# Relative bias tables gathered on the host and shifted on chip, in place of a table built on chip

## The chip, the core and the metric

One core of one Trainium2 chip runs the whole program. The metric is device microseconds (us) of one execution, the median of several runs. TensorE (PE) does the matrix work, VectorE (DVE), ScalarE (ACT) and GpSimd (POOL) the elementwise work, and SyncE (SP) issues most of the transfers, which run on 16 DMA engines. Each engine carries out its instructions in order and waits on semaphores for the others.

## The reference

One step of an encoder with two layers, over a prompt of 1024 tokens and 8 x 16 sample tokens. Layer 0 is sliding-window attention with a distance penalty; layer 1 is chunked attention over shared K and V with a learned bias per head on the clipped relative distance. Each is followed by a squared-ReLU MLP. What matters here is the bias of layer 1:

```
def relpos_bias(q_pos, k_pos, table):
    rel = jnp.clip(q_pos[:, None] - k_pos[None, :], -MAX_REL, MAX_REL) + MAX_REL
    bias = table.astype(jnp.float32)[:, rel]
    return jnp.where(band_mask(q_pos, k_pos, LEFT_CHUNKS_B)[None], bias, NEG)
...
s = jnp.einsum('bqhgd,bkhd->bhgqk', qg, k) * (HEAD_DIM ** -0.5) + bias
p = jax.nn.softmax(s, axis=-1)
```

The table has 16 heads x 257 distances. A key that is 128 or more behind its query always takes the last entry, the "edge". Softmax doesn't change when the same number is added to a whole row, so a kernel may use table minus edge, and then far keys need no bias at all.

## The kernel before, in words

Tokens go in tiles of 128: eight prompt tiles and one of samples (ST). The stages follow one another on PE: attention of layer 0, output projection, up and down products of the MLP, and the same for layer 1. Every product is made in split form (a high part and the rest), so that each weight or activation block passes through ACT (L128, the high part) and DVE (L134, the rest) or, for the attention's weights, through POOL and DVE (L190). In the down stage, blocks of activations a come from DRAM (hd) and blocks of weights r are added to w; 40 steps of 36 matmuls follow one another.

The bias of layer 1 is made in the first down stage, at step RANK = 20 of 40 (`prep_bias`, `spread_bias`). SP loads the table (tb, L1202). DVE fills fr (L1204) and a tile big of 128 x 1152 (L1205), and forms edge minus table, reversed, in fr (L1206). SP stores fr to DRAM (fd, L1210), then copies it 128 times to rd (L1212, 2048 rows of 1536 bytes), so that a read with a pitch one number short of a row gives a shifted table (`fsrc`). Sixteen small transfers (L1230, L1231) put pieces of it into big for the samples, and L1235 stores big to biasSd.

Layer 1's attention reads them. `bias_b(j)` loads the table of one KV head (four heads, 128 x 1024) from rd with L1627 and masks a corner with a memset (L1628); j = 0 and 1 at the start, 2 and 3 half way. `score_b` and `score_w` add it to the scores, which are made with negated queries, take the minimum, and let ACT compute exp of the minimum minus the score. Each of 16 sample units (`unit`) loads 128 x 288 from biasSd (L558) and does the same in L599 to L600.

The attention opens with K and V of tiles 0, 1 and ST (`K1`): PE projects (L219 to L221), DVE and POOL normalize (kssq L288, kms L290, krs on POOL, kw L293, ks L304), and DVE makes hl, the low part of a tile's hidden state (L134), of the next tile. Meanwhile SP loads four blocks of w_q (L146, raw) and spills hidden states to DRAM (hTd, L1456), all on one queue. A scheduler that simulates the program puts each engine's instructions in order; in the opening those of the attention have a raised priority. In the down stage the order is held by explicit dependences (`behind`, `chain`).

Of the kernel before, what the change touches and what calls it, by code (L numbers as in the profile page):

```python
# [8 lines left out]
F32 = mybir.dt.float32  # L9
F32R = mybir.dt.float32r  # L10
AF = mybir.ActivationFunctionType
ALU = mybir.AluOpType
# [4 lines left out]
P = 128  # L17
# [5 lines left out]
H = 16  # L23
KV = 4
G = 4
# [5 lines left out]
RANK = 20  # L31
# [21 lines left out]
BIG = 1e30  # L53
NREL = 257
# [12 lines left out]
def shape_constants():  # L67
    c = np.zeros((P, C_W), np.float32)
    q = np.arange(P)[:, None]
    k = np.arange(2 * P)[None, :]  # L70
    ba = np.abs(q + P - k).astype(np.float32)
    ba[:64, 192:256] = BIG
    ba[64:, 0:64] = BIG
    c[:, C_BA : C_BA + 256] = ba
    sa = np.full((P, 288), BIG, np.float32)
    i = np.arange(16)
    for hh in range(4):
        for b in range(2):
# [9 lines left out]
    return c  # L88


def halves(t):
# [3 lines left out]
class Build:  # L95
# [443 lines left out]
    def unit(self, up, small, layer, bp, j, v8, gq8, cache_k, cache_v):  # L539
        nc = self.nc  # L540
# [13 lines left out]
        if layer == 0:  # L554
            bias = self.cst[:, C_SA : C_SA + 288]
        else:
            bias = up.tile([P, 288], F32, tag="ub", name="ub")
            nc.sync.dma_start(bias, self.biasSd[j])  # L558
        kp = kc
        self.eng("c").tensor_tensor(kp, kc, gq8.unsqueeze(1).to_broadcast([P, 2, HD]), ALU.mult)  # L560
        if "p" in self.engs:
            yield
            a, b = slice(0, 64), slice(64, 128)
# [16 lines left out]
        s = self.psum("u", [P, 288], "ps_us")  # L580
        for v in range(2):
            nc.tensor.matmul(s, qu[:, v], kb, start=(v == 0), stop=(v == 1))
        mn = small.tile([P, 1], F32, tag="smn", name="smn")
        pn = up.tile([P, P], F32, tag="pn", name="pn")
        nc.gpsimd.memset(pn, 0.0)
        p = up.tile([P, 288], F32, tag="sp", name="sp") if layer == 0 else bias
        l = small.tile([P, 1], F32, tag="sl", name="sl")
        if layer == 0:
            nc.vector.tensor_tensor_reduce(
                s, s, bias, 1.0, self.susink[:, j : j + 1], ALU.add, ALU.min, mn  # L590
            )
# [11 lines left out]
        nc.scalar.activation(p[:, 0:256], p[:, 0:256], AF.Copy, scale=li)  # L603
# [363 lines left out]
    def mlp_down(self, layer, out):  # L967
        nc = self.nc
        tt = nc.vector.tensor_tensor
        wd = self.ins["w_down"][layer].rearrange("(c g h p) n -> g h p c n", g=2, h=2, p=P)  # L970
        with ExitStack() as st:
            self.psum_pools(st, f"dn{layer}", dict(z=(2, 1), c=(6, 1)), dict(c="c"))
            kinds = dict(
                a=([P, 2, 4, 3 * P], F32R), w=([P, 2, 4, 512], F32R), r=([P, 4, 512], F32),
                s=([P, 4, 512], F32), x=([P, D], F32),
# [11 lines left out]
            for n, tags in enumerate(DOWN_HOME):  # L987
                pool = self.pool(st, f"d{n}_{layer}")
                for t in tags.split():
                    if t == "bias":  # L990
                        self.bias_tiles(pool)
                        pool.tile([P, 248], F32, tag="pad", name="pad")
                    elif t[0] == "+":
# [130 lines left out]
                    chain(z)  # L1124
            late = iter(self.late)
            for n, (s, p, g, first, final, reads, _) in enumerate(seq):
                if layer == 0 and n == RANK:
                    self.prep_bias(self.dp)
                if layer == 0 and n == RANK + 4:
                    self.spread_bias(self.dp)  # L1130
                if n + AHEAD < total:
                    load_w(n + AHEAD)
                split_h(n + 1)
# [6 lines left out]
                a, w = aa.pop(n), ws.pop(n)  # L1140
                adds, whole = {}, {}
                for o, v in reads:
                    if o not in opened:
# [3 lines left out]
                        z = take(f"o{no % 2}")  # L1147
# [3 lines left out]
                for i in range(3):  # L1151
                    if i == 2 and n + 2 in total_of:
                        chain(total_of[n + 2])
                    c = slice(i * P, i * P + P)
                    z = [
                        self.mm3(
                            banks[i], a[:, 0, k, c], a[:, 1, k, c], w[:, 0, k], w[:, 1, k],
                            first and k == 0, k == 3,
                        )
                        for k in range(4)  # L1160
                    ]
                    self.follow(z[0][0], z[-1][1])
                    for o, v in reads:
# [6 lines left out]
                        t = PARTS[o // 2][i]  # L1170
# [22 lines left out]
    def bias_tiles(self, pool):  # L1193
        self.tb = pool.tile([H, NREL], F32, tag="tb", name="tb")
        self.fr = pool.tile([H, 384], F32, tag="fr", name="fr")
        self.big = pool.tile([P, KV, 288], F32, tag="big", name="big")

    def prep_bias(self, dp):
        nc = self.nc
        with ExitStack() as st:  # L1200
            tb, fr, big = self.tb, self.fr, self.big
            a = nc.sync.dma_start(tb, self.ins["rel_bias_b"][0])  # L1202
            self.behind(self.sp, a)
            self.behind(self.dve, nc.vector.memset(fr, 0.0))  # L1204
            self.behind(self.dve, nc.vector.memset(big, BIG))  # L1205
            nc.vector.tensor_scalar(  # L1206
                fr[:, 127:383], tb[:, 256:0:-1], -1.0, tb[:, 256:257], ALU.mult, ALU.add
            )
            fd = dp.tile([H, 384], F32, tag="fd", name="fd")
            nc.sync.dma_start(fd, fr)  # L1210
            rd = dp.tile([H, P, 384], F32, tag="rd", name="rd")
            nc.sync.dma_start(rd, fd[0:H].unsqueeze(1).to_broadcast([H, P, 384]))  # L1212
            ra = rd[0:H]

            def fsrc(h, off, n, nh, hs, w):
                return bass.AP(
                    tensor=ra.tensor, offset=ra.offset + h * P * 384 + 127 + off,
                    ap=[[383, n], [hs * P * 384, nh], [1, w]],
                )

            self.fsrc = fsrc

    def spread_bias(self, dp):
        nc, big, fsrc = self.nc, self.big, self.fsrc
        for h4 in range(G):
            for b in range(2):
                r = slice(h4 * 32 + b * 16, h4 * 32 + b * 16 + 16)
                c = 256 + b * 16
                for z in (
                    nc.sync.dma_start(big[r, :, b * P : b * P + P], fsrc(h4, 0, 16, KV, G, P)),  # L1230
                    nc.sync.dma_start(big[r, :, c : c + 16], fsrc(h4, P, 16, KV, G, 16)),  # L1231
                ):
                    self.behind(self.sp, z)
        self.biasSd = dp.tile([KV, P, 288], F32, tag="biasSd", name="biasSd")
        nc.sync.dma_start(self.biasSd[0:KV].rearrange("j p c -> p j c"), big)  # L1235

    def prep_gains(self):
        nc, I = self.nc, self.ins
# [130 lines left out]
    def attention(self, layer):  # L1369
        nc, I = self.nc, self.ins  # L1370
        A = layer == 0
# [16 lines left out]
        with ExitStack() as st:  # L1388
# [4 lines left out]
            self.pad(st, f"smpad{layer}", 32 if A else 256)  # L1393
# [3 lines left out]
            self.pad(st, f"ringpad{layer}", 168 if A else 64)  # L1397
# [226 lines left out]

            def bias_b(j):
                b = ring.tile([P, G, 256], F32, tag="biasB", name="biasB", bufs=cfg["bias_bufs"])
                nc.sync.dma_start(b, self.fsrc(j * G, 0, P, G, 1, 256))  # L1627
                nc.vector.memset(b[0:64, :, 192:256], BIG)  # L1628
                self.biasB[j] = b

# [146 lines left out]
            for s in range(2 * NT):  # L1777
# [54 lines left out]
def make_plan(tail, second):  # L1832
# [16 lines left out]
AFTER = mybir.DependencyInfo(mybir.DependencyClass.NoSync, mybir.DependencyReason.DATA)  # L1849
EARLY = (300, 150, 110, 90)  # L1850
DOWN_HOME = (
    "s1", "r0", "o0", "+512", "s0", "o1", "+512", "r3", "x5", "x6", "x7", "bias", "r4", "r5", "+384", "x8", "x0", "x2", "+640",
    "a0", "x1", "x3", "x4", "r6", "a1", "a2", "w0", "w1", "r7", "r8", "r9", "r10",
)
TAIL = 6
# [56 lines left out]
```

## Time and profile before

| What | Value |
|---|---|
| Runs before | 2350.42, 2356.03, 2356.86 us (median 2356.03) |
| Span of the profiled execution, first to last instruction | 2349.6 us |
| Its own time | not listed apart; the shortest run lies 0.8 us above the span |
| PE busy | 2273.2 us, 97% |
| DVE busy | 1718.3 us, 73% |
| ACT busy | 1332.0 us, 57% |
| POOL busy | 644.7 us, 27% |
| SP's DMA queue q1 | 188816 packets, 283.58 MB, 37.8% of the 16 engines' span |
| Granted PE clock, mean | 0.993 |
| First down stage, where the bias is made | about 963 to 1017 us of the span |
| Opening of the second attention | about 1131 to 1184 us |

A row of the timeline has the start, the duration, the engine with its line, the operation, the tiles written and read, and in brackets how long the engine was idle before it and what ended that. "SPq" rows are transfers being issued. "PEclk" is the granted clock as a share of full speed. The counts of DMA packets by size sum over the 16 DMA engines; the transfers' own marks of completion, 4 bytes each, are counted among them.

### The profile page before, as it was taken

The page shows a single profiled execution, that of the slowest core. Times are in us where ns is not written, and L with a number is a line of the kernel's source. Part 1 is how long each engine was busy: PE and PEld are TensorE (multiplying, and loading weights), DVE is VectorE, ACT ScalarE, POOL GpSimd, SP SyncE. Part 2 cuts the span into 40 slices and gives each one's busy share as a digit, 9 for nine tenths or more (in the row PEclk, how much of TensorE's full clock was granted, in tenths as well). Part 3 has the DMA queues.
Part 4 walks back from the last instruction along what each step waited for, and adds up shares of the span by engine and source line. Part 5 has one row for each costly group of instructions (what it writes and reads, how often), then busy time and mean ns, then how long its engine had stood idle before and what let it go on. Part 6 is the DMA issues. An engine that isn't in the chain of part 4 may idle for free.

```text
span 2349.6 us, 33397 instructions
## 1 busy us (share of the span) xinstructions
PE 2273.2 (97%) x11429; PEld 1899.3 (81%) x11429; DVE 1718.3 (73%) x3075; ACT 1332.0 (57%) x2684; POOL 644.7 (27%) x950
## 2 busy tenths in 40 slices
PE   8999999899999999999899899999899999999999
PEld 6787877788888888778778778887888888888887
DVE  6888786766656578898577776877666566678987
ACT  3777674555555555344377666665655555555443
POOL 4434332313213111002433444345132132210011
PEclk9999999999999999999999999999999999999999
DMA  7435546234334687848654656555243343877567
GB/s 262 128 103 177 166 141 208 89 122 162 132 112 152 218 231 174 272 142 206 191 157 114 190 151 180 166 172 186 72 162 132 114 160 113 276 212 197 183 165 198
DMA packets 226715, 392.70 MB, mean 167 GB/s; under 512 B 51592, under 2 KB 126288, under 8 KB 226448
## 3 DMA queue, kind: packets, MB, share of 16 engines
q1 hardware_dynamic: 188816, 283.58, 37.8%
q0 software_dynamic: 36432, 102.26, 16.0%
q10 hardware_dynamic: 1296, 4.72, 0.5%
q8 instruction: 90, 1.47, 0.3%
q14 instruction: 81, 0.66, 0.1%
HBM read 236.51 MB, written 156.85 MB: 167 GB/s over the span
## 4 chain that ended last, share of the span: by engine, by line
PE 73%; DVE 11%; DMA 8%; ACT 3%; issue 2%; POOL 2%; SPq 1%; ACTq 0%; DVEq 0%; POOLq 0%
PE ps_c L745 7%; PE ps_c L746 7%; PE ps_c L747 7%; PE ps_x L745 5%; PE ps_x L747 5%; PE ps_x L746 5%; PE ps_mm L219 3%; PE ps_mm L221 3%; PE ps_mm L220 3%; PE ps_y L747 2%; PE ps_y L746 2%; PE ps_y L745 2%; PE ps_tr L326 2%; DMA a<-hd 2%; DVE w L134 1%
## 5 line engine op out<-in xcount | busy, mean ns | idle before, releaser
L746 PE MATMUL ps_c<-w,a 128*128 128x512 f32 x960 | 374.0, 390 | 3.9 <-DVE w L134 3.9
L745 PE MATMUL ps_c<-w,a 128*128 128x512 f32 x960 | 374.1, 390 | 3.2 <-ACT o L1165 1.7
L747 PE MATMUL ps_c<-w,a 128*128 128x512 f32 x960 | 373.5, 389 | 0.0
L910 POOL DMA_DIRECT2D hd<-h x272 | 149.4, 552 | 594.3 <-ACT h L819 378.4
L745 PEld LDWEIGHTS ps_c<-w,a 128*128 128x128 f32 x960 | 180.2, 188 | 42.9 <-issue 2.7
L746 PEld LDWEIGHTS ps_c<-w,a 128*128 128x128 f32 x960 | 180.2, 188 | 42.7 <-DVE w L134 5.6
L747 PEld LDWEIGHTS ps_c<-w,a 128*128 128x128 f32 x960 | 180.2, 188 | 37.4
L128 ACT CAST a<-a 128x1536 fp32r<-128x1536 f32 x80 | 118.6, 1483 | 154.6 <-DMA a<-hd 154.6
L219 PE MATMUL ps_mm<-w,hh 128*128 128x512 f32 x432 | 173.9, 403 | 12.8 <-ACT hh L128 5.4
L221 PE MATMUL ps_mm<-w,hl 128*128 128x512 f32 x432 | 172.4, 399 | 1.4 <-DVE hl L134 1.2
L220 PE MATMUL ps_mm<-w,hh 128*128 128x512 f32 x432 | 171.4, 397 | 0.3
L134 DVE TENSOR_TENSOR a<-a 128x1536 fp32r<-128x1536 f32 x80 | 140.6, 1757 | 40.6 <-ACT a L128 40.5
L745 PE MATMUL ps_x<-sx,w 128*128 128x512 f32 (+1 forms) x408 | 157.8, 387 | 4.5 <-ACT h L866 2.7
L128 ACT CAST w<-ru 128x512 fp32r<-128x512 f32 (+1 forms) x160 | 109.9, 708 | 84.4 <-PE ps_y L746 32.0
L128 ACT CAST w<-s 128x2048 fp32r<-128x2048 f32 x56 | 107.1, 1912 | 88.2 <-DVE s L1062 78.8
L747 PE MATMUL ps_x<-sx,w 128*128 128x512 f32 (+1 forms) x408 | 154.2, 378 | 0.3 <-DVE w L134 0.3
L746 PE MATMUL ps_x<-sx,w 128*128 128x512 f32 (+1 forms) x408 | 154.1, 378 | 0.0
L134 DVE TENSOR_TENSOR w<-s,w 128x2048 fp32r<-128x2048 f32 x56 | 128.2, 2289 | 32.3 <-ACT w L128 32.0
L1182 POOL DMA_DIRECT2D xp<-o x28 | 36.2, 1294 | 411.6 <-ACT o L1165 391.0
L134 DVE TENSOR_TENSOR w<-ru,w 128x512 fp32r<-128x512 f32 (+1 forms) x160 | 129.7, 813 | 14.8 <-ACT w L128 14.7
L134 DVE TENSOR_TENSOR ptl<-ps_tr,pth 128x512 fp32r<-128x512 f32 x180 | 122.5, 685 | 21.2 <-ACT pth L128 17.5
L818 ACT ACTIVATE h<-h 128x512 f32<-128x512 f32 (+1 forms) x102 | 61.9, 607 | 122.1 <-DVE h L868 93.0
(274 smaller groups left out, 6152.9 us busy)
## 6 DMA issues: line engine op xcount, KB each, us to landing
a<-hd SPq DMA_DIRECT2D x80, 768.0 KB, 6.2
hd<-h POOLq DMA_DIRECT2D x272, 192.0 KB, 2.5
ru<-in_w_up SPq DMA_DIRECT2D x64, 512.0 KB, 3.9
r<-in_w_down SPq DMA_DIRECT2D x32, 1024.0 KB, 9.8
xp<-o POOLq DMA_DIRECT2D x28, 768.0 KB, 9.5
o<-oTd SPq DMA_DIRECT2D x50, 256.0 KB, 3.9
x<-xp SPq DMA_DIRECT2D x23, 512.0 KB, 5.5
xp<-xo SPq DMA_DIRECT2D x18, 512.0 KB, 2.9
```

The costliest lines, as they stand in the source:

```text
L128: a = nc.scalar.copy(hi, src)
L134: return a, e.tensor_tensor(lo, src, hi.bitcast(F32), ALU.subtract)
L219: nc.tensor.matmul(ps, a, w[:, 0, k, :], start=(k == 0), stop=False)
L220: nc.tensor.matmul(ps, a, w[:, 1, k, :], start=False, stop=False)
L221: self.lp = nc.tensor.matmul(ps, b, w[:, 0, k, :], start=False, stop=(k == KC - 1))
L326: self.lp = nc.tensor.transpose(pt[:, i, :], get(i), self.ident)
L745: a = mm(ps, ah, bh, start=first, stop=False, skip_group_check=True)
L746: mm(ps, ah, bl, start=False, stop=False, skip_group_check=True)
L747: return a, mm(ps, al, bh, start=False, stop=last, skip_group_check=True)
L818: a = nc.scalar.activation(t, src, AF.Relu)
L910: return lambda p, z: self.nc.gpsimd.dma_start(self.hd[c // 4][:, p, c % 4], z)
L1182: nc.gpsimd.dma_start(dst, z, accum_op=ALU.add)
```

## The change

The host gathers two tables from the input, without arithmetic other than a fill value: rel_p, per KV head 128 x 4 x 256 numbers, and rel_s, per KV head 128 x 288. `prep_bias`, `spread_bias` and `bias_tiles` go; their place in SBUF is kept by a gap of 2048 numbers. `bias_b` loads rel_p, and DVE subtracts it from the edge, relf, on chip. relf, 128 x 16, is loaded once at the start of the second attention, repeated over all partitions. The sample unit adds rel_s in its plain sign, takes the maximum, and negates it with one more small instruction.

```diff
             bias = up.tile([P, 288], F32, tag="ub", name="ub")
-            nc.sync.dma_start(bias, self.biasSd[j])
+            nc.sync.dma_start(bias, self.ins["rel_s"][j])
...
-            nc.vector.tensor_tensor_reduce(s, s, bias, 1.0, BIG, ALU.add, ALU.min, mn)
-            nc.scalar.activation(p, s, AF.Exp, bias=mn, scale=-1.0, accum_out=l)
+            nc.vector.tensor_tensor_reduce(s, bias, s, 1.0, -BIG, ALU.subtract, ALU.max, mn)
+            nm = small.tile([P, 1], F32, tag="snm", name="snm")
+            nc.vector.tensor_scalar(nm, mn, -1.0, None, ALU.mult)
+            nc.scalar.activation(p, s, AF.Exp, bias=nm, accum_out=l)
...
-                if layer == 0 and n == RANK:
-                    self.prep_bias(self.dp)
-                if layer == 0 and n == RANK + 4:
-                    self.spread_bias(self.dp)
...
-                nc.sync.dma_start(b, self.fsrc(j * G, 0, P, G, 1, 256))
+                nc.sync.dma_start(b, I["rel_p"][j])
+                edge = relf[:, j * G : j * G + G].unsqueeze(2).to_broadcast([P, G, 256])
+                nc.vector.tensor_tensor(b, edge, b, ALU.subtract)
                 nc.vector.memset(b[0:64, :, 192:256], BIG)
...
                 self.biasB = {}
+                relf = ring.tile([P, H], F32, tag="relf", name="relf")
+                nc.sync.dma_start(relf, I["rel_bias_b"][0, :, NREL - 1].partition_broadcast(P))
                 bias_b(0)
...
+def relative_tables(rel):
+    q = np.arange(P)[:, None]
+    at = np.clip(q + P - np.arange(2 * P)[None, :], -128, 128) + 128
+    p = rel[:, at].reshape(KV, G, P, 2 * P).transpose(0, 2, 1, 3)
```

The order of instructions moves at three places that the prediction speaks of. First, SP's queue at the opening of the second attention, from gq on (raw is w_q, hTd the spilled hidden states, biasB the table of one KV head). Before:

```order
L627 DMA gq<-in_g_q_b 128x64
L1627 DMA biasB<-rd 128x4x256
L1456 DMA hTd_114<-hh 128x512
L1456 DMA hTd_114<-hl 128x512
L1456 DMA hTd_115<-hh 128x512
L146 DMA raw<-in_w_q_b 128x2x512
```

After, with the line numbers of the changed kernel:

```order
L643 DMA gq<-in_g_q_b 128x64
L1641 DMA relf<-in_rel_bias_b 128x16x1
L1592 DMA biasB<-in_rel_p 128x1024
L1421 DMA hTd_114<-hh 128x512
L1421 DMA hTd_114<-hl 128x512
L160 DMA raw<-in_w_q_b 128x2x512
```

The load of relf stands ahead of the first table, and the third block of w_q has moved ahead of a spill.

Second, DVE at the same time, from the first K tile's sum of squares on (kssq, kms, kw and ks belong to the K normalization, VS to V, hl to the sample tile's hidden state). Before:

```order
L288 TENSOR_REDUCE kssq<-kw 128x4
L1628 MEMSET biasB 64x4x64
L290 TENSOR_SCALAR kms<-kssq,ex 128x4
L293 TENSOR_TENSOR kw<-kw,krs 128x256
L304 TENSOR_TENSOR ks<-kw,gkq 128x256
L279 SCALAR_TENSOR_TENSOR VS<-ps_mm,rx,VS 128x4x64
L134 TENSOR_TENSOR hl<-ps_n,hh 128x512 x2
```

After:

```order
L302 TENSOR_REDUCE kssq<-kw 128x4
L1594 TENSOR_TENSOR biasB<-relf,biasB 128x1024
L304 TENSOR_SCALAR kms<-kssq,ex 128x4
L1595 MEMSET biasB 64x4x64
L293 SCALAR_TENSOR_TENSOR VS<-ps_mm,rx,VS 128x4x64
L307 TENSOR_TENSOR kw<-kw,krs 128x256
L148 TENSOR_TENSOR hl<-ps_n,hh 128x512
```

The subtraction has come in ahead of kms, and VS stands ahead of kw.

Third, DVE in the first down stage, where the table was made (x are output tiles, a and w the split blocks). Before:

```order
L1204 MEMSET fr 16x384
L1205 MEMSET big 128x1152
L134 TENSOR_TENSOR a_9985<-a_9985 128x1536
L134 TENSOR_TENSOR w_10050<-s_9994,w_10050 128x2048
L1062 TENSOR_TENSOR s_10053<-r_9935,r_9987 128x2048
L1206 TENSOR_SCALAR fr<-tb 16x256
```

After, the three rows on fr and big are gone and the others stand in the same order; on SP the loads and stores of tb, fd, rd, big and biasSd are gone likewise. In the second attention all engines' rows are interleaved anew; outside it nothing else moves.

More of the change, by code (lines that the diff above doesn't have):

```diff
@@ L88, in shape_constants @@
     return c
+def relative_tables(rel):
+    q = np.arange(P)[:, None]
+    at = np.clip(q + P - np.arange(2 * P)[None, :], -128, 128) + 128
+    p = rel[:, at].reshape(KV, G, P, 2 * P).transpose(0, 2, 1, 3)
+    s = np.full((KV, P, 288), -BIG, np.float32)
+    i = np.arange(16)[:, None]
+    for hh in range(G):
+        for b in range(2):
+            r = slice(hh * 32 + b * 16, hh * 32 + b * 16 + 16)
+            s[:, r, b * P : (b + 1) * P] = rel[hh::G][:, at[:16, :P]]
+            s[:, r, 256 + b * 16 : 256 + b * 16 + 16] = rel[hh::G][:, i - i.T + 128]
+    return np.ascontiguousarray(p), s
 def halves(t):
@@ L989, in mlp_down @@
                 for t in tags.split():
[L990 to L993, printed above, removed]
+                    if t[0] == "+":
                         pool.tile([P, int(t[1:])], F32, tag="gap", name="gap")
@@ L1191, in mlp_down @@
                         load_h(m)
[L1193 to L1235, printed above, removed]
     def prep_gains(self):
@@ L1392, in attention @@
             small = self.pool(st, f"sm{layer}", 4 if A else 3)
-            self.pad(st, f"smpad{layer}", 32 if A else 256)
+            self.pad(st, f"smpad{layer}", 32 if A else 232)
             hpool = self.pool(st, f"ht{layer}")
@@ L1396, in attention @@
             ring = self.pool(st, f"ring{layer}")
-            self.pad(st, f"ringpad{layer}", 168 if A else 64)
+            self.pad(st, f"ringpad{layer}", 168 if A else 48)
             apool = self.pool(st, f"att{layer}", 2)
@@ L1851 @@
 DOWN_HOME = (
-    "s1", "r0", "o0", "+512", "s0", "o1", "+512", "r3", "x5", "x6", "x7", "bias", "r4", "r5", "+384", "x8", "x0", "x2", "+640",
+    "s1", "r0", "o0", "+512", "s0", "o1", "+512", "r3", "x5", "x6", "x7", "+2048", "r4", "r5", "+384", "x8", "x0", "x2", "+640",
     "a0", "x1", "x3", "x4", "r6", "a1", "a2", "w0", "w1", "r7", "r8", "r9", "r10",
@@ L1898 @@
     given["eye"] = np.eye(P, dtype=np.float32)
+    given["rel_p"], given["rel_s"] = relative_tables(np.asarray(inputs["rel_bias_b"])[0])
     for name, a in given.items():
```

## The prediction

> **What bounds the kernel now.** I read the page first, for who is busy and what the chain that ended last is made of.
>
> ```profile
> span 2349.6 us, 33397 instructions
> PE 2273.2 (97%) x11429; PEld 1899.3 (81%) x11429; DVE 1718.3 (73%) x3075; ACT 1332.0 (57%) x2684; POOL 644.7 (27%) x950
> PE 73%; DVE 11%; DMA 8%; ACT 3%; issue 2%; POOL 2%; SPq 1%; ACTq 0%; DVEq 0%; POOLq 0%
> ```
>
> TensorE (PE) is busy 97% of the span and none of its work changes. So an edit can only move the 76.4 us in which PE is idle (2349.6 − 2273.2): it gains at most the idle time that it caused, and it loses whatever it puts between PE and its operands. Next I asked for busy time by stretch, at the places that the change touches: the first down stage, the opening of the second attention, and its steady part.
>
> ```profile
> 955.00:1030.00 75.00, 70.77 (x309) 57.32 (x308) 64.75 (x55) 29.52 (x20) 0.00 (x0) 1.00 0.66 220
> 1142.00:1150.00 8.00, 8.00 (x31) 6.42 (x30) 5.27 (x11) 1.83 (x5) 1.37 (x2) 0.81 0.99 303
> 1150.00:1158.00 8.00, 8.00 (x42) 6.71 (x41) 5.55 (x16) 2.85 (x10) 3.63 (x6) 1.00 0.99 324
> 1200.00:1620.00 420.00, 403.14 (x2206) 334.92 (x2206) 318.19 (x868) 278.39 (x766) 173.80 (x234) 0.99 0.53 160
> ```
>
> The columns are length, then PE, PEld, DVE, ACT and POOL busy, the granted clock, the DMA share and GB/s. In the down stage around the removed preparation PE is busy 70.77 of 75 us. In the opening (1142 to 1158) PE is busy throughout, and so are the DMA engines, at 0.99: every packet put into the queue there delays what stands behind it. In the steady part PE is idle for 16.9 of 420 us.
>
> **What the removal gives.** These are the times at which PE waited between 955 and 1030, from the timeline:
>
> ```profile
> 972.85 0.50 PE L746 MATMUL ps_c<-w,a 128*128 128x512 f32 x1 [1.06 <-DVE w L134]
> 989.75 0.47 PE L745 MATMUL ps_c<-w,a 128*128 128x512 f32 x1 [0.52 <-DVE x L1177]
> 1000.16 0.50 PE L746 MATMUL ps_c<-w,a 128*128 128x512 f32 x1 [1.74 <-DVE w L134]
> ```
>
> And these are the rows of the preparation, with the one on which the third wait hangs:
>
> ```profile
> 967.40 0.38 DVE L1204 MEMSET fr<- 16x384 f32 x1
> 967.97 1.02 DVE L1205 MEMSET big<- 128x1152 f32 x1 [0.19 <-issue]
> 994.63 1.48 ACT L128 CAST a<-a 128x1536 fp32r<-128x1536 f32 x1 [3.41 <-DMA a<-hd]
> rd<-fd SPq DMA_DIRECT2D x1, 3072.0 KB, 15.7
> ```
>
> The two memsets took VectorE (DVE) from 967.40 to 968.99, 1.59 us ahead of the split of w whose end released PE at 972.85. Without them that wait of 1.06 us is covered. The 0.52 us at 989.75 has the same origin, since DVE ran late from there on: taken as gone as well. The 1.74 us at 1000.16 come from an activation block a that ACT got only at 994.63, while the 3 MB copy rd<-fd shared the queue with it: gone too. The gain is 1.06 + 0.52 + 1.74 = 3.3 us. Its bounds are 0 (something else is late next) and 3.3 (PE wasn't idle for longer). The other removed transfers (tb, fd, sixteen big<-rd, biasSd) have no PE wait behind them.
>
> **What the addition costs: one small load in a full queue.** The new relf load takes one number per head out of rows that lie 1028 bytes apart and repeats it for 128 partitions. That is 128 x 16 = 2048 pieces of 4 bytes, 8 KB in all. SP issues it behind gq and ahead of the first bias table, a split block of hidden state, and the last two blocks of w_q. The trace has no such load of 2048 pieces, so I bound it by counted packets. First the four ssink loads at the start (4-byte pieces repeated over partitions, 512 in all), the stretch in their midst, and then gk and gq at the very place of relf (rows repeated over partitions), and one load of 256 rows that aren't repeated:
>
> ```profile
> DMA packets 880, 0.74 MB, mean 143 GB/s; under 512 B 603, under 2 KB 603, under 8 KB 880
> ...
> DMA packets 135, 0.00 MB, mean 0 GB/s; under 512 B 135, under 2 KB 135, under 8 KB 135
> ...
> DMA packets 565, 0.53 MB, mean 313 GB/s; under 512 B 299, under 2 KB 505, under 8 KB 564
> ...
> GB/s 0 0 0 0 0 0 0 0 0 0 26 85 119 85 128 188 196 230 197 205 205 213 137 120 35 290 0 0 0 0 0 0 0 0 0 0 0 0 0 0
> DMA packets 273, 0.07 MB, mean 61 GB/s; under 512 B 272, under 2 KB 272, under 8 KB 272
> ```
>
> - ssink, from 16.5 to 21.7 us: 603 packets under 512 bytes in 5.2 us, 116 per us, so relf would hold the queue for 2048 / 116 = 17.7 us.
> - In its midst, 17.75 to 19.5: 135 packets in 1.75 us, 77 per us, which would make 26.5 us.
> - gk and gq, 1146.5 to 1148.2: 299 in 1.7 us, 176 per us, so 11.6 us.
> - kc, 78.8 to 80.0: 272 in the 16 of 40 slices of 0.03 us that moved bytes, 567 per us, so 3.6 us.
>
> I take 11.6 us, from gk and gq: relf is repeated over partitions as they are, and stands next to them on the same queue. The ends 3.6 and 17.7 stay for the range. That a slow small load holds back what is behind it shows at the start:
>
> ```profile
> 16.12 0.39 SPq L146 DMA_DIRECT2D raw<-in_w_qkv_a  x1
> 16.87 0.35 SPq L1456 DMA_DIRECT2D hTd<-hh  x1
> 22.32 0.16 DVE L1367 TENSOR_TENSOR susink<-ssink,rsl 128x4 f32<-128x4 f32 x1 [3.39 <-DMA ssink<-in_sink_a]
> ```
>
> The block raw was issued at 16.12 and the spill hTd at 16.87, yet from 17.75 to 19.5 not one of the 135 packets was as large as 512 bytes: ssink's pieces were in front.
>
> [...]
>
> **Who waits for it.** DVE takes the first subtraction (biasB from relf, 128x1024) just ahead of kms of the first K tile. DVE works in order, so everything behind that waits too: the K normalizations, VS, and hl of the sample tile, which PE needs next. The rows of before at that place:
>
> ```profile
> 1143.96 0.70 SPq L1627 DMA_DIRECT2D biasB<-rd  x1
> DMA to landing us min/median/max: 5.7/6.1/6.5
> 1151.18 0.27 DVE L1628 MEMSET biasB<- 64x256 f32 x1
> 1151.38 0.20 DVE L290 TENSOR_SCALAR kms<-kssq,ex 128x4 f32<-128x4 f32 x1
> 1152.70 0.42 DVE L293 TENSOR_TENSOR kw<-kw,krs 128x256 f32<-128x256 f32 x1 [1.13 <-POOL krs L292]
> 1154.62 0.48 DVE L279 SCALAR_TENSOR_TENSOR VS<-ps_mm,rx,VS 128x256 fp32r<-128x256 f32 x1 [1.03 <-ACT VS L278]
> 1155.11 1.29 DVE L134 TENSOR_TENSOR hl<-ps_n,hh 128x512 fp32r<-128x512 f32 x2
> 955.07 1.75 DVE L134 TENSOR_TENSOR a<-a 128x1536 fp32r<-128x1536 f32 x1
> ```
>
> The table lands at 1143.96 + 6.1 = 1150.1, about 1 us before DVE asks for it. With relf ahead it lands at 1150.1 + D. The subtraction takes about 1.2 us (128x512 took 0.65 each in the pair at 1155.11, 128x1536 took 1.75). Behind it come kms 0.20, the memset 0.27, VS 0.48 and kw 0.42, with some 0.35 of waiting for POOL in between, 2.9 us in all. So hl starts at 1153.0 + D instead of 1155.11: the delay is D − 2.1 us, because DVE had two waits there (1.13 and 1.03) that the new wait swallows. PE was never idle in this stretch and its row of work is in order, so it stops for 11.6 − 2.1 = 9.5 us. The last w_q blocks are delayed as well, through the same queue, but no further than this.
>
> A stop that long costs PE more than its length:
>
> ```profile
> 1140.86 0.76 PE L219 MATMUL ps_mm<-w,hh 128*128 128x512 f32 x1 [5.43 <-ACT hh L128]
> 1145.66 0.40 PE L219 MATMUL ps_mm<-w,hh 128*128 128x512 f32 x1
> 1146.35 0.40 PE L219 MATMUL ps_mm<-w,hh 128*128 128x512 f32 x1
> 1180.08 0.89 PE L433 MATMUL ps_sn<-KT,qT 128*128 128x128 f32 x6 [2.24 <-DVE qT L134]
> 1170.00:1184.00 14.00, 11.76 (x71) 10.09 (x70) 8.99 (x22) 7.16 (x15) 5.24 (x4) 1.00 0.35 106
> ```
>
> After 5.43 us of idleness the first four groups of three matmuls took 1145.66 − 1140.86 = 4.80 us, where the next one took 0.69: 4.80 − 4 x 0.69 = 2.0 us lost, at a granted clock of 0.81. After 2.24 us of idleness the clock stayed at 1.00. So 2.0 us more where the stop is nearer 5 us, nothing where it is under 2.2.
>
> **The small edits.** The other three subtractions are 1.2 us of DVE each:
>
> ```profile
> 1381.42 0.27 DVE L1628 MEMSET biasB<- 64x256 f32 x1 [0.27 <-DMA biasB<-rd]
> 1393.96 0.27 DVE L1628 MEMSET biasB<- 64x256 f32 x1 [2.14 <-DMA biasB<-rd]
> 1150.21 0.15 DVE L204 TENSOR_SCALAR vx<-xssq 128x1 f32<-128x1 f32 x1
> PE ps_utp L607 <- ACT ub L603: 0.3, 1, 0.3
> ```
>
> For the later two tables DVE waited already, up to 2.14 us, and the list of PE's waits names no biasB: covered by PE's queued work, 0; without that cover 2.4 us. The second subtraction stands between two halves of the last w_q block, behind the same queue: inside the 9.5. The negation in each of 16 sample units costs 0.15 us as the 128x1 row; PE waited only once on that chain, 0.3 us: I take 0.5 us, bounds 0 and 2.4. Reading in_rel_s instead of biasSd moves the same bytes: 0. The scheduler also interleaves the second attention anew; PE's work is the same, and of its 16.9 us idle there a third may come or go: 0, give or take 5.
>
> **The sum.** −3.3 + 9.5 + 2.0 + 0.5 = +8.7 us on the profiled execution. Its span is 2349.6; the shortest of the three runs, 2350.42, lies 0.8 above that, and the median, 2356.03, 6.4 above it. Added to the median: 2364.7 us. About 0.3%, 7.1 us, is what a measurement of this kernel can tell from no change.
>
> **Rivals.**
> - *The small load is quick* (not slower than before): relf goes at kc's pace, 3.6 us. Then hl is only 1.5 us late, PE's clock stays up, and −3.3 + 1.5 + 0.5 = −1.3 gives 2354.7; wholly hidden it is −2.8 and 2353.2. For it: relf's 16 sources lie 1028 bytes apart, where ssink's lie next to each other. Against: none of the repeated loads ran at that pace. It decides below a relf of 5 us; the loss passes 0.3% only above 10 us (D − 2.9 = 7.1). [...]
> - *ssink's own pace*: D = 17.7, so −3.3 + 15.6 + 2.0 + 0.5 = +14.8 and 2370.8. For it: the same piece size and kind. Against: it ran at the very start.
> - *The new interleaving decides*: half of the 16.9 us idle in the steady part gained or doubled up. With a quick relf that is −2.8 − 8.4, 2344.8; on top of the forecast +17.1, 2373.1. Nothing in the trace speaks for either sign.
>
> **How the numbers follow.** Chances: forecast (D from 8 to 15, so +5 to +12) 0.48; quick load 0.27; ssink's pace 0.15; interleaving 0.10, half to each sign. Of the forecast's share two thirds lie above 10 us, 0.31 slower and 0.17 within 0.3%. Slower: 0.31 + 0.15 + 0.05 = 0.51. Within: 0.17 + 0.27 = 0.44. Faster: 0.05. The range runs from a little under the hidden load to a little over ssink's pace with some loss: 2352 to 2373.
>
> **What would show it.** Right: DVE waiting around 1150 for relf or biasB for some 10 us, PE idle about as long before the sample tile's K projection and a granted clock under 1 behind it, and about 2 us or less of PE idle between 955 and 1030. Wrong: a wait at that subtraction under 3 us (quick load), PE waits in the down stage that stay, or a gap in the opening that is made up again by 1200.

## The result and the profile after

The change took 2367.03 us in the median (2361.89 to 2371.51, six runs), the kernel before 2356.29 beside it: a ratio of 1.0045 with a 95% interval from 1.0029 to 1.0062, slower by 10.7 us. The forecast was 2364.7. The time came out about as forecast, but the profile shows that it got there by another way. The page of the changed kernel, its span, its engines' busy time and the chain of work that ended last:

```profile
span 2363.6 us, 33385 instructions
PE 2282.2 (97%) x11429; PEld 1904.6 (81%) x11429; DVE 1721.5 (73%) x3092; ACT 1332.7 (56%) x2684; POOL 647.7 (27%) x950
PE 79%; DVE 9%; DMA 6%; ACT 2%; issue 2%; SPq 1%; POOL 0%; ACTq 0%; DVEq 0%; POOLq 0%
```

The profiled execution took 2365.41 us. TensorE's busy time rose by 9.0 us (from 2273.2) with the same 11429 matmuls: the same work ran on a slower clock for a while (a granted clock of 0.990 in the mean, where before had 0.993). The next views ask in which stage. First the down stage and the edge's load, by windows (same columns as in the prediction), then the packets of the second window:

```profile
955.00:1030.00 75.00, 74.51 (x329) 61.33 (x328) 69.62 (x55) 33.44 (x22) 0.00 (x0) 1.00 0.51 174
1139.70:1142.80 3.10, 3.10 (x16) 2.55 (x15) 3.10 (x4) 0.50 (x1) 1.38 (x2) 1.00 0.55 61
```

```profile
DMA packets 2274, 0.19 MB, mean 61 GB/s; under 512 B 2244, under 2 KB 2244, under 8 KB 2273
```

TensorE got through 329 matmuls in the 75 us where it did 309 before: 20 x 74.51 / 329 = 4.5 us gained, as an estimate. And the 2244 small packets around the edge's load, which has 128 x 16 = 2048 pieces, passed in 3.1 us with TensorE busy all the time; 2034 of them were of 4 bytes. The first K product on TensorE, SP's queue and the first subtraction, from the timeline:

```profile
1132.94 0.47 PE L233 MATMUL ps_mm<-w,hh 128*128 128x512 f32 x1 [1.47 <-ACT hh L142]
...
1138.27 0.43 SPq L1641 DMA_DIRECT2D relf<-in_rel_bias_b  x1
1138.74 3.49 SPq L1592 DMA_DIRECT2D biasB<-in_rel_p  x1
...
1146.32 1.23 DVE L1594 TENSOR_TENSOR biasB<-relf,biasB 128x1024 f32<-128x1024 f32 x1 [1.84 <-DMA biasB<-in_rel_p]
```

VectorE waited 1.84 us for the first table, not some 10, and TensorE didn't stop for it. TensorE's wait ahead of the first K product shrank to 1.47 us from 5.43. So far the changed kernel is ahead. It loses all of that, and more, in the steady part of the second attention. I take that part from the first ps_sn product to the first product of the output projection, and behind it to the 200th product of the next up stage: both hold the same numbers of matmuls in all of these kernels, give or take missing records. Before, then after:

```profile
1180.10:1618.10 438.00, 421.13 (x2316) 350.88 (x2317) 332.71 (x923) 292.14 (x808) 180.35 (x249) 0.99 0.53 162
1618.10:1730.30 112.20, 103.26 (x606) 89.88 (x605) 80.16 (x121) 65.75 (x130) 38.77 (x44) 0.97 0.40 134
```

```profile
1171.30:1628.60 457.30, 430.48 (x2315) 356.06 (x2316) 334.52 (x941) 292.14 (x808) 183.32 (x249) 0.97 0.51 155
1628.60:1744.00 115.40, 104.21 (x605) 91.05 (x604) 78.66 (x121) 65.70 (x130) 40.53 (x44) 0.96 0.38 130
```

The steady part takes 457.3 us in place of 438.0. Of the 19.3 us, 457.30 - 430.48 - (438.00 - 421.13) = 9.9 are idleness, and 430.48 - 421.13 = 9.4 are the same matmuls on a granted clock of 0.97 in place of 0.99. The profile doesn't say whether the added work or the order did this; the experiments have to.

### The profile page after: what moved, and what is told of

It reads as the page before. It is cut to its first block, busy times and chain, and to the rows that moved or that the text cites. A ratio compares the mean times of both kernels' runs of the same rounds, so it can differ in the third digit from the quotient of the medians.

```text
span 2363.6 us, 33385 instructions
## 1 busy us (share of the span) xinstructions
PE 2282.2 (97%) x11429; PEld 1904.6 (81%) x11429; DVE 1721.5 (73%) x3092; ACT 1332.7 (56%) x2684; POOL 647.7 (27%) x950
## 3 DMA queue, kind: packets, MB, share of 16 engines
q8 instruction: 90, 1.47, 0.3%
## 4 chain that ended last, share of the span: by engine, by line
PE 79%; DVE 9%; DMA 6%; ACT 2%; issue 2%; SPq 1%; POOL 0%; ACTq 0%; DVEq 0%; POOLq 0%
PE ps_c L761 8%; PE ps_c L763 8%; PE ps_c L762 8%; PE ps_x L761 5%; PE ps_x L763 5%; PE ps_x L762 5%; PE ps_mm L233 3%; PE ps_mm L234 3%; PE ps_mm L235 3%; PE ps_y L763 2%; PE ps_tr L340 2%; PE ps_y L761 2%; PE ps_y L762 2%; PE ps_mm L190 2%; PE ps_mm L192 1%
## 5 line engine op out<-in xcount | busy, mean ns | idle before, releaser
L142 ACT CAST pth<-ps_tr 128x512 fp32r<-128x512 f32 x180 | 105.1, 594 | 50.2 <-PE ps_tr L340 40.8
```

Of the source, the lines that this page charges most:

```text
L142: a = nc.scalar.copy(hi, src)
```

## The experiments

Two theories stood against each other. *Order*: the scheduler interleaved the second attention anew, and in the new order TensorE stops more often; the added work is nearly free. *Work*: the subtractions, the negations and the edge's load cost the time. A third, *table*, was kept beside them: the tables gathered on the host land later than those built on chip. To part them I tied rows to a given order: between neighbours in the wanted order of TensorE and of VectorE a dependence is added that carries no semaphore, so that it holds the scheduler alone and makes nothing wait on the chip. Other engines stay free, and nearly fall into the same order.

```diff
+    def pin(self):
+        by = {i.name: i for b in self.nc.main_func.blocks for i in b.instructions}
+        for rows in PINS.values():
+            for a, b in zip(rows, rows[1:]):
+                self.tc.add_manual_dep(by[f"I-{b}"], f"I-{a}", AFTER, reason="pin")
```

All results together. "Moved" is the smallest number of TensorE's rows to take out so that the others stand as in the kernel before. Ratios are to runs of the kernel before on the same chip, whose medians were 2355.65 to 2357.82 us.

| Kernel | Moved | Median us | Ratio, 95% interval |
|---|---|---|---|
| the change | 395 | 2367.03 | 1.0045 [1.0029, 1.0062] |
| removal alone | 9 | 2347.12 | 0.9955 [0.9939, 0.9970] |
| the change, old order | 0 | 2349.68 | 0.9966 [0.9952, 0.9980] |
| removal alone, the change's order | 395 | 2367.08 | 1.0043 [1.0026, 1.0059] |
| the change, unit in its old form | 272 | 2362.31 | 1.0017 [1.0005, 1.0029] |
| the change, TensorE's old order only | 0 | 2352.91 | 0.9984 [0.9969, 0.9998] |
| the change, old order in the late part | 300 | 2355.60 | 0.9995 [0.9982, 1.0008] |
| the change, old order in the early part | 95 | 2358.21 | 1.0002 [0.9985, 1.0018] |
| the change, old order, four edge loads | 0 | 2358.85 | 1.0015 [1.0000, 1.0029] |
| before, one more row per unit | 535 | 2369.12 | 1.0058 [1.0044, 1.0072] |
| the same, old order | 0 | 2354.04 | 0.9994 [0.9982, 1.0006] |
| additions alone | 535 | 2372.47 | 1.0067 [1.0052, 1.0082] |
| the change, negation on GpSimd | 342 | 2357.03 | 1.0004 [0.9995, 1.0014] |

**Work and order taken apart.** The removal alone, in nearly the old order (the fill value of the samples' table and two paddings change with it and aren't shown):

```diff
-                edge = relf[:, j * G : j * G + G].unsqueeze(2).to_broadcast([P, G, 256])
-                nc.vector.tensor_tensor(b, edge, b, ALU.subtract)
...
-                relf = ring.tile([P, H], F32, tag="relf", name="relf")
-                nc.sync.dma_start(relf, I["rel_bias_b"][0, :, NREL - 1].partition_broadcast(P))
...
-            nc.vector.tensor_tensor_reduce(s, bias, s, 1.0, -BIG, ALU.subtract, ALU.max, mn)
-            nm = small.tile([P, 1], F32, tag="snm", name="snm")
-            nc.vector.tensor_scalar(nm, mn, -1.0, None, ALU.mult)
-            nc.scalar.activation(p, s, AF.Exp, bias=nm, accum_out=l)
+            nc.vector.tensor_tensor_reduce(s, s, bias, 1.0, BIG, ALU.add, ALU.min, mn)
+            nc.scalar.activation(p, s, AF.Exp, bias=mn, scale=-1.0, accum_out=l)
```

> The removal alone: the table is no longer built in the first down stage and the attention loads the gathered tables, but there is no load of the edge, no subtraction and no negation, and the sample unit keeps its old form (so the shift by the edge and the sign of the bias are left out of the computation). TensorE's rows stand as before, but for 9 moved ones. Order theory (the new interleaving costs some 19 us in the second attention): the down stage gives its 5 us and nothing is lost later, 2351 us, from 2346 to 2353. Work theory (the four subtractions, the 16 negations and the edge's load cost the 19 us): the same, 2351. Table theory (the tables gathered on the host land later than the ones built on chip): 2360 or more.

The whole change with the rows of before (PINS from the kernel before):

> The whole change, with the rows of TensorE and VectorE in the second attention tied to the order that they had before (the added rows stand at their places in the program). Order theory: 2351 us plus at most 3 for the added work, 2350 to 2355. Work theory: as slow as the change itself, 2364 to 2369. Table theory: 2364 to 2369 too.

And the removal alone with the rows of the change (PINS from the changed kernel):

> The removal alone as above (shift and sign left out), with the rows of TensorE and VectorE in the second attention tied to the order that the whole change has. Order theory: nearly as slow as the whole change, 2363 to 2368. Work theory: 2351, as the removal alone. Table theory: 2360 or more, as the removal alone.

2347.12, 2349.68 and 2367.08 us: the order theory holds in all three (the second lies 0.3 us under its 2350 to 2355), and the work and table theories fall. The change's order costs 20.0 us (2367.08 - 2347.12) with none of the added work in it and 17.3 (2367.03 - 2349.68) with all of it, and the added work costs 2.6 us (2349.68 - 2347.12) in the old order, which these intervals, of about 0.14% to each side, don't tell from nothing. The steady part and what follows it, in the whole change with the old order:

```profile
1172.30:1607.10 434.80, 419.40 (x2317) 347.89 (x2317) 335.49 (x941) 292.34 (x808) 179.70 (x249) 1.00 0.53 163
1607.10:1718.30 111.20, 103.34 (x604) 89.98 (x603) 79.58 (x121) 65.62 (x130) 38.53 (x44) 0.97 0.41 135
```

and in the removal alone with the change's order:

```profile
1179.60:1625.40 445.80, 424.28 (x2317) 350.96 (x2317) 331.56 (x923) 291.18 (x808) 180.62 (x249) 0.99 0.52 159
1625.40:1743.40 118.00, 105.08 (x605) 91.60 (x603) 78.35 (x121) 65.34 (x130) 39.30 (x44) 0.94 0.38 127
```

The columns of VectorE (335.49 against 331.56 us) show that the first does more work and the second less, and yet the first takes 546.0 us for both stretches and the second 563.8. These are single executions, and the first of them took 2341.08 us, 8.6 under its median, so the size of the gap is read from the medians. One thing stays open: the change itself takes 572.7 us for these stretches, 8.9 more than the removal in the same order, but reaches them 8.3 us earlier. So that the added work is nearly free is shown for the old order only.

**What a worse order looks like.** TensorE's waits of over 1 us between 1300 and 1352 in the changed kernel:

```profile
1305.47 0.63 PE L340 MATMUL ps_tr<-identr,p 128*128 128x128 f32 x4 [1.69 <-DVE KT L148]
1314.99 0.62 PE L447 MATMUL ps_sf<-KT,qT 128*128 128x384 f32 x2 [1.25 <-ACT p L484]
1319.53 0.77 PE L233 MATMUL ps_mm<-w,hh 128*128 128x512 f32 x1 [2.85 <-DMA hh<-hTd]
1334.37 0.50 PE L233 MATMUL ps_mm<-w,hh 128*128 128x512 f32 x1 [1.08 <-DMA hh<-hTd]
1350.75 0.53 PE L596 MATMUL ps_us<-kb,qu 128*128 128x288 f32 x2 [1.46 <-DVE KT L148]
```

With the old order the same stretch has two:

```profile
1313.36 0.47 PE L233 MATMUL ps_mm<-w,hh 128*128 128x512 f32 x1 [1.45 <-DMA hh<-hTd]
1325.24 0.47 PE L233 MATMUL ps_mm<-w,hh 128*128 128x512 f32 x1 [1.16 <-DMA hh<-hTd]
```

The first of the five can be read off VectorE's timeline. KT is the low part of a K tile, in two halves; the transposes of p (ps_tr) at 1305.47 start once the second is done. In the changed kernel:

```profile
1300.86 0.42 DVE L148 TENSOR_TENSOR KT<-ps_q,KT 64x256 fp32r<-64x256 f32 x1
1301.50 1.17 DVE L204 SCALAR_TENSOR_TENSOR w<-raw,gcol,w 128x512 fp32r<-128x512 f32 x1 [0.23 <-POOL w L199]
1302.76 0.11 DVE L471 MEMSET ps_sf<- 64x64 f32 x1
1302.78 0.47 DVE L493 TENSOR_TENSOR l<-l 128x2 f32<-128x2 f32 x1
1303.17 0.77 DVE L204 SCALAR_TENSOR_TENSOR w<-raw,gcol,w 128x512 fp32r<-128x512 f32 x1
1303.86 0.47 DVE L293 SCALAR_TENSOR_TENSOR VS<-ps_mm,rx,VS 128x256 fp32r<-128x256 f32 x1
1304.25 0.54 DVE L472 TENSOR_REDUCE mnb<-ps_sf 128x1 f32<-128x384 f32 x1
1304.71 0.15 DVE L494 RECIPROCAL li<-l 128x2 f32<-128x2 f32 x1
1304.89 0.43 DVE L148 TENSOR_TENSOR KT<-ps_q,KT 64x256 fp32r<-64x256 f32 x1
```

and in the old order:

```profile
1298.13 0.42 DVE L148 TENSOR_TENSOR KT<-ps_q,KT 64x256 fp32r<-64x256 f32 x1
1298.47 0.47 DVE L475 CUSTOM_DVE_ANT_0 ps_sn<-ps_sn,biasB,mnb 128x256 f32<-128x256 f32 x1
1298.97 0.08 DVE L475 DVE_READ_ACCUMULATOR2_ANT mnb<- 128x1 f32 x1
1299.08 0.43 DVE L148 TENSOR_TENSOR KT<-ps_q,KT 64x256 fp32r<-64x256 f32 x1
```

The halves start 0.95 us apart in the old order. In the new one seven rows stand between them, two of them parts of the weights' preparation (L204), and they start 4.03 us apart. None of these rows is new; they only stand elsewhere. All five waits come back in the removal with the change's order, which has none of the added work: 1.69, 1.23, 3.27, 1.13 and 1.83 us.

**Which engine, and which part of the stage.** TensorE's rows alone tied to the old order:

> The whole change, with TensorE's rows alone tied to the order that they had before; VectorE's are left to the scheduler (93 of them moved against before, where the whole change moves 278). If TensorE's order is what costs: as fast as with both tied, 2348 to 2354 us. If it is VectorE's order: between 2356 and 2367. Work theory (by now unlikely): 2367.

2352.91 us: 14.1 of the 17.3 us that both together bring come back with TensorE's rows alone. Next, one part of the stage in the old order, the other in the new (PINS cut where the two orders hold the same rows so far):

> The whole change; TensorE and VectorE keep the new order up to about 1508 us of the span and the old one behind it, to the end of the second attention. By the profiles, the stretch from there into the next up stage took 231.3 us in the whole change and 220.5 with the old order. If the loss is spread over the stage, this kernel gains that part, 10.8 of 2367: 2356, from 2353 to 2360. If all of it comes from the early part (where the first tables and the first units stand): 2367. If all of it comes from the late part: 2350.

> The whole change; TensorE and VectorE keep the old order up to about 1508 us of the span and the new one behind it. If the loss is spread: what the late part doesn't explain, 17.3 - 10.8 = 6.5 us less than 2367, so 2360.5, from 2357 to 2364, and the gains of this kernel and of its counterpart add up to some 17. If the early part is all: 2350; if the late part is all: 2367.

The late part brings 2367.03 - 2355.60 = 11.4 us (10.8 were expected from the profiles), the early part 8.8 (6.5 expected); the sum is 20.2 where both bring 17.3, as near as the intervals allow. So the loss is spread over the stage. Waits come and go with their part. In the kernel whose early part is new, the wait of 1.69 us of the changed kernel is back:

```profile
1311.38 0.63 PE L340 MATMUL ps_tr<-identr,p 128*128 128x128 f32 x4 [1.69 <-DVE KT L148]
```

and in the one whose late part is new, the longest stop stands at the end of the output projection (the change itself stops there for 4.7 us),

```profile
1651.54 1.12 PE L708 MATMUL ps_n<-identr,x 128*128 128x128 f32 x4 [6.10 <-DVE sx L148]
```

where the change in the old order waits less than half as long:

```profile
1634.02 1.25 PE L708 MATMUL ps_n<-identr,x 128*128 128x128 f32 x8 [2.80 <-DVE sx L148]
```

**What sets the order.** The sample unit in its old form, without the negation:

```diff
-            nc.vector.tensor_tensor_reduce(s, bias, s, 1.0, -BIG, ALU.subtract, ALU.max, mn)
-            nm = small.tile([P, 1], F32, tag="snm", name="snm")
-            nc.vector.tensor_scalar(nm, mn, -1.0, None, ALU.mult)
-            nc.scalar.activation(p, s, AF.Exp, bias=nm, accum_out=l)
+            nc.vector.tensor_tensor_reduce(s, s, bias, 1.0, BIG, ALU.add, ALU.min, mn)
+            nc.scalar.activation(p, s, AF.Exp, bias=mn, scale=-1.0, accum_out=l)
```

> The whole change but for the sample unit, which keeps its old form without the negation (the sign of the samples' bias is left out). The scheduler is free and gives a third order, 272 rows of TensorE away from before's. Unit theory (the negation in the chain of each of 16 units costs): 2351 to 2356. Subtraction theory (the four subtractions cost): 2364 to 2369. Order theory: no value follows from the work; something between 2348 and 2370, with its idle time at other places than the whole change.

2362.31 us, neither the unit's nor the subtractions' value: a third order with a time of its own. The sharper test puts one small row into each unit of the kernel before and touches nothing else but a padding that makes room for it:

```diff
             nc.vector.tensor_tensor_reduce(s, s, bias, 1.0, BIG, ALU.add, ALU.min, mn)
+            nm = small.tile([P, 1], F32, tag="snm", name="snm")
+            nc.vector.tensor_scalar(nm, mn, 1.0, None, ALU.mult)
-            nc.scalar.activation(p, s, AF.Exp, bias=mn, scale=-1.0, accum_out=l)
+            nc.scalar.activation(p, s, AF.Exp, bias=nm, scale=-1.0, accum_out=l)
```

> The kernel before with nothing else than one more row on VectorE in each of the 16 sample units (the minimum is copied, 128x1, and the copy is read by the exponential). The scheduler is free; 535 of TensorE's rows move against before. Work theory: 16 rows of 0.15 us, 2356 to 2359. Order theory: the time leaves that of before by more than the rows can cost, and as the orders other than before's were slower so far, 2362 to 2375.

> The same extra row in each sample unit, with the rows of TensorE and VectorE tied to the order that they had before. Both theories: 2356 to 2359, the price of the rows alone.

2369.12 us with the scheduler free, 2354.04 with the rows tied (2 under the expected 2356 to 2359, and no different from before by its interval): 16 rows of some 0.15 us cost nothing that can be measured, and the order that they bring about costs 15 us. The first three waits of over 1 us behind 1300 us in the first of the two are those of the change:

```profile
1316.18 0.63 PE L326 MATMUL ps_tr<-identr,p 128*128 128x128 f32 x4 [1.59 <-DVE KT L134]
1325.70 0.62 PE L433 MATMUL ps_sf<-KT,qT 128*128 128x384 f32 x2 [1.10 <-ACT p L470]
1330.34 0.77 PE L219 MATMUL ps_mm<-w,hh 128*128 128x512 f32 x1 [2.95 <-DMA hh<-hTd]
```

The additions without the removal (table built on chip; then the edge, the subtractions and the new unit):

> The additions alone: the table is still built in the first down stage, and the edge's load, the four subtractions and the new form of the sample unit come on top (the edge is taken off twice and the samples' sign is left wrong). Its order is nearly that of the kernel with one more row: 29 rows of TensorE apart. Order theory: the same time as that kernel, within 3 us. Work theory: 5 to 15 us above before, and clearly above that kernel.

2372.47 us, 3.4 above the kernel with one more row, 29 of whose rows it has moved: just outside the 3 us that the order theory gave, within what the two intervals allow. The last one moves the negation to another engine:

```diff
-            nc.vector.tensor_scalar(nm, mn, -1.0, None, ALU.mult)
+            nc.gpsimd.tensor_scalar(nm, mn, -1.0, None, ALU.mult)
```

> The whole change with the negation on GpSimd in place of VectorE; the scheduler is free and gives yet another order, 342 rows of TensorE away from before's. Order theory: no value follows from the work; between 2350 and 2370, and not the 2367 of the change but by chance. If the negation's place in VectorE's queue was what cost: 2352 or less.

2357.03 us: the same work but for 16 tiny rows, yet another order, and 10 us less than the change. As the negation cost nothing in the old order, its place in VectorE's queue isn't the cause.

**The price of the edge's load.** Four loads in a row in the old order, all else in place (the rows of VectorE, TensorE and ScalarE are the same; a padding makes room):

```diff
-                relf = ring.tile([P, H], F32, tag="relf", name="relf")
-                nc.sync.dma_start(relf, I["rel_bias_b"][0, :, NREL - 1].partition_broadcast(P))
+                relf4 = ring.tile([P, 4 * H], F32, tag="relf", name="relf")
+                for n in range(4):
+                    relf = relf4[:, n * H : n * H + H]
+                    nc.sync.dma_start(relf, I["rel_bias_b"][0, :, NREL - 1].partition_broadcast(P))
```

> The whole change in the old order (TensorE and VectorE tied), with the load of the edge issued four times in a row ahead of the first table (the last one is used). It prices the load and tests the chain that the prediction built on it: first table late, first subtraction late, hl of the sample tile late, TensorE stops. If one load holds the queue for 2.8 us, as the trace of the change shows, and the chain is right: the table comes 8.4 us later, TensorE stops for about 8 and restarts slowly (2), so 2349.7 + 10 = 2360, from 2356 to 2363. If one load takes the 11.6 us of the prediction: 2349.7 + 35 or more, above 2380. If a late table hurts nobody: 2350.

2358.85 us, 9.2 more than with one load. The rows of that kernel: SP's queue, the first subtraction and TensorE's stop; then two windows, the whole opening (from the last product of the down stage to the first ps_sn) and the ten microseconds of the stop:

```profile
1143.67 0.43 SPq L643 DMA_DIRECT2D gq<-in_g_q_b  x1
1144.15 8.01 SPq L1650 DMA_DIRECT2D relf<-in_rel_bias_b  x4
...
1159.32 1.23 DVE L1601 TENSOR_TENSOR biasB<-relf,biasB 128x1024 f32<-128x1024 f32 x1 [8.67 <-DMA biasB<-in_rel_p]
...
1164.53 0.69 PE L276 MATMUL ps_q<-identr,ks 128*128 128x128 f32 x2 [8.94 <-DVE ks L318]
```

```profile
1135.50:1188.70 53.20, 40.36 (x179) 32.55 (x177) 25.91 (x55) 13.76 (x32) 15.23 (x19) 0.87 0.60 166
...
1155.00:1165.00 10.00, 1.06 (x6) 0.64 (x4) 3.36 (x7) 0.10 (x1) 3.84 (x5) 0.63 0.91 297
```

With one load, gq, the subtraction and the opening:

```profile
1137.63 0.42 SPq L643 DMA_DIRECT2D gq<-in_g_q_b  x1
...
1145.67 1.23 DVE L1600 TENSOR_TENSOR biasB<-relf,biasB 128x1024 f32<-128x1024 f32 x1 [1.66 <-DMA biasB<-in_rel_p]
```

```profile
1129.10:1172.30 43.20, 38.80 (x178) 31.22 (x176) 25.16 (x55) 13.85 (x31) 15.49 (x19) 0.96 0.68 204
```

The subtraction starts 15.65 us after gq is issued in place of 8.04: three more loads put it off by 7.6 us, 2.5 each. VectorE's wait, TensorE's stop and the slower clock behind it (0.72 from 1165 to 1170) all appear as the prediction's chain had them; only TensorE's stop falls on the transposes of ks, not on the sample tile's hl.

## Why the prediction was right in its number and wrong in its way

- *Down stage, "the gain is 1.06 + 0.52 + 1.74 = 3.3 us".* The mechanism was right in the main, the size too small: 20 more matmuls in the same 75 us are 4.5 us. The bound of 3.3 overlooked that the prediction's own row has 75.00 - 70.77 = 4.2 us of idleness: a third wait for the split of w, 0.91 us at 1017.68, wasn't in its list. And the 0.52 us, taken as gone, stayed: the changed kernel waits 0.49 us at 990.69 for the same output row x. Before's own list of TensorE's waits in that window shows 3.7 + 0.5 = 4.2 us (engine, line and what was waited for; then us in total, times, longest):

```profile
PE ps_c L746 <- DVE w L134: 3.7, 3, 1.7
PE ps_c L745 <- DVE x L1177: 0.5, 1, 0.5
```


Over the whole first down stage, from the start of its first product to that of its last, the profiles show more: 334.2 us in before and 328.8 in the change; 334.2 to 337.5 in the four kernels that build the table, 328.6 to 330.9 in the ten that don't.

- *"I take 11.6 us, from gk and gq".* This is the step that failed. The load of 2048 pieces takes 2.5 us by the four loads, some 820 per us, and 2244 small packets passed in 3.1 us. The pace of the repeated loads gk and gq, 176 packets per us, and ssink, 116, didn't carry over; that of kc, 567 per us, had been the nearest and was still too low. So 9.5 + 2.0 of the sum were not there. The rival of the quick load had this right.
- *"hl is D - 2.1 late, PE stops, and the restart costs 2.0."* Not put to the test by the change, but by the four loads: 7.6 us more delay, 10.0 us more in the opening (53.20 against 43.20), which holds the stop and the restart. The chain was right, its first number wrong. Its rule for the restart, by the length of the stop, isn't borne out: the changed kernel too has a stop of 2.24 us ahead of the first ps_sn, and behind it the clock was 0.50 for 3.4 us (last section).
- *"The negation, 0.5; the subtractions, 0."* Right within what can be measured in the old order: 2.6 us for all added work, with the edge's load, and nothing for 16 small rows by themselves.
- *"The scheduler also interleaves the second attention anew: 0, give or take 5."* The second step that failed, and the one that made the time: 17 to 20 us. The prediction took the idle time there, 16.9 us, as the measure of what could come or go. In the profiled execution it grew by 9.9, and slow matmuls behind the stops, which the measure leaves out, took 9.4 more. The rival that named the interleaving had the right cause at a chance of 0.10 and, with a quick load, gave it no case of a loss.
- *The opening.* TensorE's wait ahead of the first K product, 5.43 us in before, was 0.70 to 5.44 in these kernels, 1.1 in one that still builds the table and 5.44 in one that doesn't. So the removal isn't shown to be its cause, and what sets it stays open.

That the forecast's +8.7 came near the measured 10.7 is luck, a coincidence of two errors: a load that cost nothing on TensorE's path in place of 11.5 us, and an order that cost some 17 to 20 in place of 0. The removal by itself is worth 9.9 us (2347.12 against 2356.98 for the kernel before beside it), of which the whole down stage shows 5.4 between the profiles of before and the change and 6.8 between the means of the four and the ten kernels; where the rest comes from was not settled. The change in the old order beats both kernels, 2349.68 us. Also open: why the scheduler's answer to one small row is this order, and which of its stops costs how much.

## What to carry to other kernels

Where a scheduler sets the order, a change of any size has two prices, its work and the reordering that it sets off, and a comparison of the orders tells how far the second reaches; if hundreds of TensorE's rows move, its spread belongs in the range, and it isn't bounded by the idle time of before: the free orders with 272 to 535 moved rows that were seen here were all slower than before's order with the same or nearly the same work, by 7 to 18 us. To judge such a change, tie the rows to one order first, measure the work, and only then let the scheduler go. The price of a small load can't be taken from its neighbours in the queue (here 11.6 us by theirs, 2.5 by its own): measure it by issuing it several times.

## What the runs showed of the hardware that was not expected

The granted clock fell to 0.50 behind single stops of 1.46 and 2.24 us too. The clock records of the two traces, of before and of the change, hold two values only, 1.00 and 0.50. The falls that end within the span lasted 3.41, 6.83 or 10.24 us, and all begin on one fixed grid of 3.41 us in each trace; values between, as in the windows above, are means. Cut on that grid, the fifth wait shown above (1.46 us) and then the stop of 2.24 us ahead of the first ps_sn, both in the changed kernel:

```profile
1349.03:1352.44 3.41, 1.62 (x9) 1.06 (x8) 2.46 (x7) 0.86 (x3) 2.03 (x3) 1.00 0.34 95
1352.44:1355.86 3.42, 3.42 (x9) 2.67 (x9) 3.29 (x11) 2.41 (x8) 1.40 (x2) 0.50 0.41 102
1355.86:1359.27 3.41, 3.41 (x19) 2.79 (x19) 0.93 (x4) 2.42 (x10) 1.59 (x2) 1.00 0.15 34
...
1168.12:1171.54 3.42, 1.18 (x11) 0.86 (x8) 2.32 (x5) 2.48 (x6) 0.97 (x1) 1.00 0.63 185
1171.54:1174.95 3.41, 3.41 (x19) 3.41 (x19) 2.42 (x6) 2.60 (x5) 1.22 (x2) 0.50 0.22 82
```

TensorE was busy for 1.62 of 3.41 us and for 1.18 of 3.42, and the clock was 0.50 in the next 3.41 in both cases. Some 1.5 us were lost in each, an estimate: eight transposes ps_n took 1.93 us at 1172.37, in the later stretch of 0.50, where the same eight took 1.06 at 1180.80 in before, at 1.00; 3.41 x (1 - 1.06 / 1.93) = 1.5. In before the same stop of 2.24 us fell across two stretches, of which TensorE was busy for 2.02 of 3.42 and 2.57 of 3.41 us, and the clock stayed at 1.00. So the length of one stop didn't decide it here. The two records have 16 falls within the span, 6 in before and 10 in the change, each behind a stretch of that grid of which TensorE was busy for between 11% and 52%; the emptiest stretches behind which the clock stayed at 1.00 were busy for 47% (1.60 of 3.41 us from 49.42, in before).

Pieces of 4 bytes at a stride of 1028 bytes, repeated over partitions, went at 2048 in 2.5 us by the four loads, some 820 per us, where ssink's pieces, 16 bytes apart at their source, passed at 116 packets per us at the start of the kernel (603 in 5.2 us). Why these two differ wasn't tried.
